# Values past stationary probabilities: the attention products of a hybrid decoder trunk with a query per output row

## The chip, the cores and the metric

The kernel runs on one core of a Trainium2 chip. The metric is device time in microseconds (us) of one execution. The engines are TensorE (PE; its weight loads are listed apart as PEld), VectorE (DVE), ScalarE (ACT), GpSimd (POOL) and SyncE (SP), which issues most transfers.

## What is computed

Two layers are run over 512 rows of width 1024, in float32. Each layer has three groups of attention heads: A (sliding window of 128, 8 heads with a sink), B (4 heads that see the 128 keys an indexer chose) and C (4 heads, latent attention). All have values of width 64. Their outputs are concatenated and go through one output projection; then come a layer norm and a mixture of 16 experts of which each row uses two. What the change touches is the end of each softmax; from the reference, for group C:

```python
s = jnp.where(causal[None, None], s, -jnp.inf)
p = jax.nn.softmax(s, axis=-1)
return jnp.einsum('bhts,bshd->bthd', p.astype(v.dtype), v)
```

## The kernel before

**Order of the work.** Nothing is scheduled by the hardware or a compiler. Every piece of work is a Python generator that yields steps: an engine (or two to choose from), a guessed cost and a function that issues the instructions. A planner (`Flow.run`, L144) picks at each turn the step that can start first by its guesses, with a small weight on a priority (`PRIO`, L84), and issues it. Each engine then runs its instructions strictly in that order, and the waits between the engines follow from the data. A wrong guess does not change the order; it only makes an engine wait, or arrive late, at run time.

**Stages of a layer.** The input projection (`s_project`, L538) runs in five column chunks; each product is made of three float32r products (`mm3`, L284 to 287). Rotary embedding and transposes (`turn`, L433, whose transposes are on L440) bring queries and keys into shape. An indexer scores keys for group B (`s_index`, L705) and 16 rounds of MAX8 and MATCH_REPLACE8 on DVE (L745, L746) choose 128 of them. Sixteen quads of heads (`s_quad`, L753) do the attention: a quad is four heads for one block of 128 queries. A has eight quads, B and C four each. Then come the output projection (`s_wout`, L916, again L285 to 287), the norm and the router (`s_router`, L1021, whose small products are on L1034), the table of rows (L1133 is filler work that PE does while it waits there) and twelve passes over the experts (L1619 and L1648), whose weights stream in from memory.

**One quad before.** The number of keys nk is 128 or 256 in group A, and 128, 256, 384 and 512 in B and C for the four blocks; nj is nk/128. The scores are products on PE (L786). DVE adds the mask and takes the minimum (L772), ACT takes the exponential and the row sums (L799), DVE the reciprocal of the sums (L804). Then each of the four heads' probabilities is multiplied by the reciprocal of its row's sum, on DVE (L808) or on ACT (L809), whichever the planner expects to end first. Blocks of 128 by 128 probabilities are transposed on PE (L440), up to four into one bank, and copied out (`evac`, ACT on L281 or DVE on L282). The products with the values follow (L834). There the values, 128 keys by 64, are the stationary operand, and the transposed probabilities, 128 keys by 128 queries, move past them:

```python
b = (hh % 2) * 64
T.matmul(po[b:b + 64, (hh // 2) * P:(hh // 2 + 1) * P], vs[hh][j], q[:, j], start=j == 0, stop=j == nj - 1)
```

An output has its 64 columns of values as rows; two heads of a pair write the lower and the upper 64 rows, so each product uses half of the columns of PE's array. The products of a quad are issued in one step of four heads where nk is at most 256 (`per` is 2, so a transposing step takes two heads), and in two steps of two heads otherwise. The result already stands as the output projection wants it, with features on the rows, and is copied into `mix` (quads of A) or split into its two float32r parts (B and C, L850 on ACT and L851 on DVE).

In the trace a float32 product is two matmul records, each with a weight load of its own; a transpose and a float32r product are one record each.

Of the kernel before, what the change touches and what calls it, by code (L numbers as in the profile page):

```python
# [10 lines left out]
AF = mybir.ActivationFunctionType  # L11
OP = mybir.AluOpType
# [4 lines left out]
P = 128  # L17
# [180 lines left out]
def body(tc, sb, pp, dr, x, w_in, attn_sinks, c_q_norm_g, c_kv_norm_g, w_uq, w_ukv, w_out, ln1_g, ln1_b,  # L198
         w_router, router_bias, w_gate, w_up, w_down, ln2_g, ln2_b, rope, out):
    nc = tc.nc  # L200
    V, A, G, T, SY = nc.vector, nc.scalar, nc.gpsimd, nc.tensor, nc.sync
# [25 lines left out]
    def fixed(*shape):  # L227
        n = 1
        for d in shape:
            n *= d  # L230
        return view(take_f(n), *shape)
# [14 lines left out]
    def sel(i):  # L246
        o = ((i + 1) * i // 2 - 1) * P
        return aux.of(F32)[:, o:o + (i + 1) * P]
# [12 lines left out]
    def st(eng, cost, fn, after=None):  # L261
        return Step([(eng, cost, fn)], after)

    def pe(cost, fn, after=None):
        return st("T", cost, fn, after)

    def ve(n, fn, after=None, fast=False):
        return st("V", 0.07 + n / (1920 if fast else 960), fn, after)

    def ac(n, fn, after=None, extra=0):  # L270
        return st("A", 0.07 + n / 1200 + 0.093 * extra, fn, after)
# [22 lines left out]
    ident = fixed(P)  # L294
# [103 lines left out]
    WT = Slots([fixed(512) for _ in range((NF - used[0]) // 512)])  # L398
# [8 lines left out]
    def rshape(w, *shape):  # L407
        n = 1
        for d in shape:
            n *= d  # L410
        v = w[:, :n]
        if len(shape) == 2:
            v = v.rearrange("p (a b) -> p a b", b=shape[1])
        if len(shape) == 3:
            v = v.rearrange("p (a b c) -> p a b c", b=shape[1], c=shape[2])
        return v
# [16 lines left out]
    def turn(src, n, after=None):  # L433

        got = yield Take(PS)
        ps = got[1].rearrange("p (a b) -> p a b", b=P)

        def tr():
            for j, s in enumerate(src):
                T.transpose(ps[:n, j, :], s, ident)  # L440
        t = yield pe(0.107 * len(src), tr, after)
        return got, ps[:n, :len(src), :], t

    def turned(got, q, te, dst, dst_lo=None):

        n = q.shape[1] * P
        if dst_lo is None:
            t = yield evac(n, dst, q, [te])
        else:
            t = yield ac(n, lambda: A.activation(dst, q, AF.Copy), [te])  # L450
            t = yield ve(n, lambda: V.tensor_tensor(dst_lo, q, dst.bitcast(F32), op=OP.subtract), [t])  # L451
        PS.put(got, t)
        return t
# [24 lines left out]
    def layer(l, xready, prev_free):  # L478
# [274 lines left out]
        def s_quad(q, i, need, qs, ks, vs, mask, nk, scale, c0, sink=None):  # L753

            for e in need:
                yield e
            if mask is None:
                mask = sel(i)
            nj = nk // P
            per = 2 if nk <= 256 else 1  # L760
            nm, sm, es = smalls["nm", q], smalls["sm", q], smalls.get(("es", q))
            s = [None] * 4
            gots = yield Take(WS, 4 // per)
            groups = [(0, 2), (1, 3)] if per == 2 else [(h,) for h in range(4)]
            ahead = []

            def scores():
                g_, got, tq = ahead.pop(0)
                v, ps = rshape(gots[g_][1], per, nk), got[1]
                for a, h in enumerate(groups[g_]):  # L770
                    s[h] = v[:, a]
                    t = yield ve(nk + 60, lambda: V.tensor_tensor_reduce(  # L772
                        out=v[:, a], in0=ps[:, a * nk:(a + 1) * nk], in1=mask, op0=OP.add, op1=OP.min, scale=-scale,
                        scalar=3e38 if sink is None else sink[:, h:h + 1], accum_out=nm[:, h:h + 1]), [tq])
                PS.put(got, t)
                return t

            both = qs[0].shape[0] == 64
            for g0 in range(0, len(groups), 2 if both else 1):
                banks_ = yield Take(PS, 2 if both else 1)  # L780

                def qk():
                    for a in range(per):
                        for j, got in enumerate(banks_):
                            h = groups[g0 + j][a]
                            T.matmul(got[1][:, a * nk:(a + 1) * nk], qs[h], ks[h], start=True, stop=True)  # L786
                tq = yield pe(per * 4 * nk / 2400 + 0.2 * both, qk, [])
                for j, got in enumerate(banks_):
                    ahead.append((g0 + j, got, tq))
                while len(ahead) > (0 if both else 1):  # L790
                    t = yield from scores()
            while ahead:
                t = yield from scores()
            if sink is not None:
                t0 = yield ve(4, lambda: V.tensor_tensor(es, nm, sink, op=OP.subtract), [t])
                t0 = yield ac(4, lambda: A.activation(es, es, AF.Exp), [t0])
            ts_ = []
            for h in range(4):
                ts_.append((yield ac(nk, lambda: A.activation(s[h], s[h], AF.Exp, bias=nm[:, h:h + 1], scale=-1.0,  # L799
                                                              accum_out=sm[:, h:h + 1]), [t], 3)))  # L800
            t = ts_[-1]
            if sink is not None:
                t = yield ve(4, lambda: V.tensor_tensor(sm, sm, es, op=OP.add), [t])
            t = yield ve(4, lambda: V.reciprocal(sm, sm), [t])  # L804
            tn = []
            for h in range(4):
                tn.append((yield Step([
                    ("V", 0.12 + nk / 1920, lambda: V.tensor_scalar(s[h], s[h], sm[:, h:h + 1], None, op0=OP.mult)),  # L808
                    ("A", 0.19 + nk / 1200, lambda: A.activation(s[h], s[h], AF.Copy, scale=sm[:, h:h + 1]))], [t])))  # L809
            gpo, po = None, None  # L810
            ahead = []
            for h in range(0, 4, per):
                src = [s[h + a][:, j * P:(j + 1) * P] for a in range(per) for j in range(nj)]
                b_ = yield from turn(src, P, [tn[h + per - 1]])
                gp = yield Take(WT)
                pT = rshape(gp[1], 4, P)[:, :len(src)]
                te = yield from turned(*b_, pT)
                if per == 1:
                    WS.put(gots[h], te)
                for a in range(per):  # L820
                    ahead.append((h + a, gp if a == per - 1 else None, pT[:, a * nj:(a + 1) * nj], te))
                if len(ahead) < (4 if per == 2 else 2):
                    continue

                if po is None:
                    gpo = yield Take(PS)
                    po = gpo[1]

                def pv():
                    for x in range(0, len(ahead), 2):  # L830
                        for j in range(nj):
                            for hh, _, q, _ in ahead[x:x + 2]:
                                b = (hh % 2) * 64
                                T.matmul(po[b:b + 64, (hh // 2) * P:(hh // 2 + 1) * P], vs[hh][j], q[:, j], start=j == 0, stop=j == nj - 1)  # L834
                tp = yield pe(len(ahead) / 2 * nj * 0.22 + 0.2, pv, [v[3] for v in ahead])
                for _, g_, _, _ in ahead:
                    if g_ is not None:
                        WT.put(g_, tp)
                ahead.clear()
            if per == 2:  # L840
                for g_ in gots:
                    WS.put(g_, te)
            qsl = slice(i * P, (i + 1) * P)
            qq = po[:, :2 * P].rearrange("p (a b) -> p a b", a=2)
            if q < 8:
                yield E("idx")
                t = yield evac(2 * P, mix[:, c0:c0 + 2, qsl], qq, [tp])
            else:
                yield E("mm", len(chunks) - 1)
                yield ac(2 * P, lambda: A.activation(xh()[:, c0:c0 + 2, qsl], qq, AF.Copy), [tp])  # L850
                t = yield ve(2 * P, lambda: V.tensor_tensor(xl(c0, c0 + 2, qsl), qq, xh()[:, c0:c0 + 2, qsl].bitcast(F32),  # L851
                                                            op=OP.subtract))
                flow.set(E("mix", c0 // 2, i), t)
            PS.put(gpo, t)
            flow.set(E("quad", q), t)

        for i in range(NT):
            qi = slice(i * P, (i + 1) * P)
            k0 = max(0, i - 1) * P
            nk = (i + 1) * P - k0  # L860
# [8 lines left out]
            nk = (i + 1) * P  # L869
# [955 lines left out]
```

## Time and profile before

| | |
|---|---|
| median of 3 runs | 833.25 us (833.22 to 834.62) |
| the profiled execution: its time | 835.47 us |
| its span, first to last instruction | 833.7 us |
| mean granted clock of TensorE in it | 0.995 |
| busy over the span: PE / DVE / ACT | 97% / 64% / 41% |

The span is what all rows of the trace add up to; the profiled execution's own time has 1.8 us around it. Busy time of an engine is the union of its instructions. Matmuls overlap each other: one of them is listed with some 0.27 us although the next may start 0.1 us later, so the price of a matmul in a stream is read from the starts, not from the durations. A time such as "idle before" is that of the engine which waited, with the instruction that released it.

### The profile page before, as it was taken

The numbers are of one execution on the slowest core, as the hardware profiler recorded it, in microseconds if no ns is written. First come the engines' busy times: TensorE is split into PE (matmuls) and PEld (weight loads), VectorE is DVE, ScalarE is ACT, GpSimd is POOL, SyncE is SP. The second block draws the span as 40 slices with busy tenths as digits, with TensorE's granted clock in tenths as the row PEclk, the third lists the DMA queues.
The fourth block names the chain that finished last, engine by engine and source line by source line (L and its number), as shares of the span: only waits on it lengthen the run. The fifth ranks groups of instructions, "written<-read, shape, count | busy, mean of one in ns | idle before, by whom it ended". The sixth has DMA issues, their size and how long they took to land. (4 is left out here: it accounts for less than half of the span.)

```text
span 833.7 us, 15557 instructions
## 1 busy us (share of the span) xinstructions
PE 806.0 (97%) x5960; PEld 521.7 (63%) x5960; DVE 537.5 (64%) x1588; ACT 338.2 (41%) x852; POOL 103.2 (12%) x133
## 2 busy tenths in 40 slices
PE   7999999999999999999999999999999999999995
PEld 7878896667885333333597889776688743333332
DVE  5799999974477341123998999989644854211257
ACT  4433656974232222223155265577632232222211
POOL 1010102000003111100211001110000121111004
PEclk9999999999999999999999999999999999999998
DMA  8421350064575999997434217111762699999762
GB/s 267 151 84 49 112 207 27 26 207 172 177 262 196 353 373 377 370 366 276 176 88 164 77 51 242 37 52 27 273 232 101 213 333 366 367 375 370 278 274 101
DMA packets 118848, 171.91 MB, mean 206 GB/s; under 512 B 12005, under 2 KB 95461, under 8 KB 118768
## 3 DMA queue, kind: packets, MB, share of 16 engines
q1 hardware_dynamic: 112720, 156.12, 54.6%
q0 software_dynamic: 6048, 14.73, 4.9%
q8 instruction: 48, 0.79, 0.4%
q14 instruction: 32, 0.26, 0.1%
HBM read 152.96 MB, written 25.17 MB: 214 GB/s over the span
## 5 line engine op out<-in xcount | busy, mean ns | idle before, releaser
L285 PE MATMUL bank<-ring,ra 128*128 128x512 f32 (+4 forms) x448 | 167.0, 373 | 0.5 <-ACT fa L604 0.5
L1648 PE MATMUL bank<-fa,ra 128*32 128x512 f32 x1080 | 160.0, 592 | 0.2
L286 PE MATMUL bank<-ring,xl 128*128 128x512 f32 (+4 forms) x448 | 157.6, 352 | 0.9 <-DVE xl L451 0.9
L287 PE MATMUL bank<-ring,ra 128*128 128x512 f32 (+4 forms) x448 | 158.0, 353 | 0.0
L281 ACT ACTIVATE fa<-bank 128x256 f32<-128x256 f32 (+3 forms) x172 | 86.1, 514 | 108.2 <-PE bank L440 80.2
L1524 DVE TENSOR_TENSOR fa<-fa,bank 128x256 f32<-128x256 f32 x24 | 10.1, 421 | 160.3 <-ACT fa L1523 160.3
L1648 PEld LDWEIGHTS bank<-fa,ra 128*32 128x32 f32 x1080 | 47.6, 109 | 76.6 <-issue 65.6
L285 PEld LDWEIGHTS bank<-ring,ra 128*128 128x128 f32 x448 | 85.0, 190 | 14.9 <-issue 7.1
L287 PEld LDWEIGHTS bank<-ring,ra 128*128 128x128 f32 x448 | 84.8, 189 | 8.2
L286 PEld LDWEIGHTS bank<-ring,xl 128*128 128x128 f32 x448 | 85.2, 190 | 7.4 <-DVE xl L451 1.3
L1619 PE MATMUL bank<-fa 128*32 128x512 f32 x504 | 80.0, 595 | 1.4 <-DVE fa L282 0.6
L440 PE MATMUL bank<-fa 128*128 128x128 f32 (+1 forms) x456 | 71.9, 282 | 7.4 <-DMA fa<-in_x_dram 5.7
L473 ACT ACTIVATE ring<-fa 128x1024 fp32r<-128x1024 f32 (+4 forms) x56 | 49.5, 898 | 55.4 <-PE bank L286 49.8
L440 PEld LDWEIGHTS bank<-fa 128*128 128x128 f32 (+1 forms) x456 | 55.4, 144 | 24.4 <-issue 10.5
L1523 ACT ACTIVATE fa<-bank 128x256 f32<-128x256 f32 x24 | 9.2, 385 | 151.1 <-PE bank L1648 144.5
L1648 PE MATMUL bank<-ring,ra 128*32 128x512 f32 x360 | 67.1, 592 | 0.0
L474 DVE TENSOR_TENSOR ring<-fa,ring 128x1024 fp32r<-128x1024 f32 (+4 forms) x56 | 58.0, 1043 | 7.4 <-ACT ring L473 7.3
L1514 DVE TENSOR_SCALAR ra<-bank,fa 128x128 f32<-128x128 f32 x110 | 41.8, 408 | 27.9 <-ACT ra L1513 24.5
L746 DVE MATCH_REPLACE8 aux<-fa,aux 128x256 f32<-128x256 f32 (+2 forms) x96 | 51.9, 545 | 0.0
L745 DVE MAX8 fa<-aux 128x8 f32<-128x256 f32 (+2 forms) x96 | 50.6, 551 | 0.1
L1513 ACT ACTIVATE ra<-bank,fa 128x128 f32<-128x128 f32 x82 | 33.7, 458 | 41.1 <-DVE ra L1514 36.6
L786 PE MATMUL bank<-fa 64*128 64x256 f32 (+7 forms) x256 | 47.4, 413 | 0.0
(218 smaller groups left out, 1235.5 us busy)
## 6 DMA issues: line engine op xcount, KB each, us to landing
fa<-in_w_gate_dram SPq DMA_DIRECT2D x45, 512.0 KB, 9.8
fa<-in_w_up_dram SPq DMA_DIRECT2D x45, 512.0 KB, 9.8
fa<-in_w_down_dram SPq DMA_DIRECT2D x21, 1024.0 KB, 10.5
xl<-in_w_down_dram SPq DMA_DIRECT2D x9, 1024.0 KB, 10.5
fa<-in_w_out_dram SPq DMA_DIRECT2D x8, 1024.0 KB, 5.7
yd<-fa SPq DMA_DIRECT2D x16, 512.0 KB, 8.7
ring<-in_w_gate_dram SPq DMA_DIRECT2D x15, 512.0 KB, 6.8
ring<-in_w_up_dram SPq DMA_DIRECT2D x15, 512.0 KB, 11.9
```

What stands on the lines that cost most here:

```text
L281: return Step([("A", 0.05 + n / 1200, lambda: A.activation(dst, src, AF.Copy)), ("V", 0.12 + n / 960, lambda: V.tensor_copy(dst, src))], a ...
L285: T.matmul(ps, xh, wh, start=start, stop=False)
L286: T.matmul(ps, xl, wh, start=False, stop=False)
L287: T.matmul(ps, xh, wl, start=False, stop=stop)
L440: T.transpose(ps[:n, j, :], s, ident)
L473: yield Step([("A", 0.09 + n / 1200, lambda: A.activation(hv, raw, AF.Copy))], None)
L474: t = yield ve(n, lambda: V.tensor_tensor(lv, raw, hv.bitcast(F32), op=OP.subtract))
L745: yield ve(nk, lambda: V.max(m8, sc))
L746: yield ve(nk, lambda: V.match_replace(sc, m8, sc, MARK))
L786: T.matmul(got[1][:, a * nk:(a + 1) * nk], qs[h], ks[h], start=True, stop=True)
L1619: T.matmul(a[1][cs], ht[:, j, cs], E("raw", e, 2).got[1][:, j, n * 512:(n + 1) * 512], start=j == 0, stop=j == 1)
L1648: T.matmul(acc[1][cs], gh[:, 4 * u + j, cs], E("raw", e, u).got[1][:, j], start=u + j == 0, stop=u + j == 4)
```

## The change

The quad's end is turned around. The exponentials are transposed as they are, without the division. In the products the transposed exponentials (128 keys by 128 queries) are the stationary operand and the values (128 keys by 64) move; an output has a query per row and, for four heads, 256 columns. These rows are multiplied by the reciprocals in one DVE instruction per quad, which writes them over the last buffer of transposed exponentials; two transposes on PE turn them into the other half of the same bank, and from there the result is copied as before. The steps of the products now come once per transposing step.

```diff
--- before.py
+++ after.py
@@ -802,46 +802,43 @@
             if sink is not None:
                 t = yield ve(4, lambda: V.tensor_tensor(sm, sm, es, op=OP.add), [t])
             t = yield ve(4, lambda: V.reciprocal(sm, sm), [t])
-            tn = []
-            for h in range(4):
-                tn.append((yield Step([
-                    ("V", 0.12 + nk / 1920, lambda: V.tensor_scalar(s[h], s[h], sm[:, h:h + 1], None, op0=OP.mult)),
-                    ("A", 0.19 + nk / 1200, lambda: A.activation(s[h], s[h], AF.Copy, scale=sm[:, h:h + 1]))], [t])))
-            gpo, po = None, None
-            ahead = []
+
+            td = t
+            gpo, po, spare = None, None, None
             for h in range(0, 4, per):
                 src = [s[h + a][:, j * P:(j + 1) * P] for a in range(per) for j in range(nj)]
-                b_ = yield from turn(src, P, [tn[h + per - 1]])
+                b_ = yield from turn(src, P, [ts_[h + per - 1]])
                 gp = yield Take(WT)
                 pT = rshape(gp[1], 4, P)[:, :len(src)]
                 te = yield from turned(*b_, pT)
                 if per == 1:
                     WS.put(gots[h], te)
-                for a in range(per):
-                    ahead.append((h + a, gp if a == per - 1 else None, pT[:, a * nj:(a + 1) * nj], te))
-                if len(ahead) < (4 if per == 2 else 2):
-                    continue
-
                 if po is None:
                     gpo = yield Take(PS)
                     po = gpo[1]
 
                 def pv():
-                    for x in range(0, len(ahead), 2):
+                    for a in range(per):
                         for j in range(nj):
-                            for hh, _, q, _ in ahead[x:x + 2]:
-                                b = (hh % 2) * 64
-                                T.matmul(po[b:b + 64, (hh // 2) * P:(hh // 2 + 1) * P], vs[hh][j], q[:, j], start=j == 0, stop=j == nj - 1)
-                tp = yield pe(len(ahead) / 2 * nj * 0.22 + 0.2, pv, [v[3] for v in ahead])
-                for _, g_, _, _ in ahead:
-                    if g_ is not None:
-                        WT.put(g_, tp)
-                ahead.clear()
+                            T.matmul(po[:, (h + a) * 64:(h + a + 1) * 64], pT[:, a * nj + j], vs[h + a][j], start=j == 0, stop=j == nj - 1)
+                tp = yield pe(per * nj * 0.115, pv, [te])
+                if h + per < 4:
+                    WT.put(gp, tp)
             if per == 2:
                 for g_ in gots:
                     WS.put(g_, te)
+
+            rows = rshape(gp[1], 4, 64)
+            t = yield ve(2 * P, lambda: V.tensor_tensor(rows, po[:, :2 * P].rearrange("p (a b) -> p a b", b=64), sm[:, :, None].to_broadcast([P, 4, 64]),
+                                                        op=OP.mult), [tp, td])
+
+            def tr():
+                for j in range(2):
+                    T.transpose(po[:, (2 + j) * P:(3 + j) * P], gp[1][:, j * P:(j + 1) * P], ident)
+            tp = yield pe(0.214, tr, [t])
+            WT.put(gp, tp)
             qsl = slice(i * P, (i + 1) * P)
-            qq = po[:, :2 * P].rearrange("p (a b) -> p a b", a=2)
+            qq = po[:, 2 * P:].rearrange("p (a b) -> p a b", a=2)
             if q < 8:
                 yield E("idx")
                 t = yield evac(2 * P, mix[:, c0:c0 + 2, qsl], qq, [tp])
```

## Rows read from the trace of the kernel before

**Rows 1.** The page, busy time over the whole span: share, number of instructions

```profile
PE 806.0 (97%) x5960; PEld 521.7 (63%) x5960; DVE 537.5 (64%) x1588; ACT 338.2 (41%) x852; POOL 103.2 (12%) x133
```

**Rows 2.** Windows: both attention stretches and the output projection behind the first, all engines

```profile
core 0: us, PE busy (x) PEld busy (x) DVE busy (x) ACT busy (x) POOL busy (x), PEclk, DMA share, GB/s
70.00:200.00 130.00, 127.47 (x887) 99.21 (x886) 112.20 (x386) 85.30 (x258) 13.32 (x21) 1.00 0.35 117
200.00:245.00 45.00, 44.79 (x287) 38.40 (x284) 24.67 (x72) 14.17 (x23) 2.32 (x4) 1.00 0.53 182
...
478.00:612.00 134.00, 131.49 (x908) 102.25 (x907) 117.08 (x397) 87.29 (x256) 13.85 (x23) 1.00 0.35 120
```

**Rows 3.** The longest wait of PE, first attention stretch: total us, times, longest

```profile
PE bank L834 <- DVE ring L282: 1.0, 2, 0.7
```

**Rows 4.** Windows of L834 alone, then its groups with the idle time before them

```profile
70.00:200.00 130.00, 20.72 (x272) 15.12 (x272) 1.00 0.35 117
478.00:612.00 134.00, 19.97 (x272) 14.90 (x272) 1.00 0.35 120
...
L834 PE MATMUL bank<-fa 128*64 128x128 f32 x290 | 26.7, 279 | 0.7 <-DVE fa L282 0.4 <-ACT fa L281 0.3
...
L834 PE MATMUL bank<-ring,fa 128*64 128x128 f32 x254 | 24.3, 281 | 2.3 <-DVE ring L282 1.8 <-ACT ring L281 0.5
```

**Rows 5.** Timeline of PE: one step of L834 between projections (start, duration)

```profile
93.49 1.10 PE L834 MATMUL bank<-fa 128*64 128x128 f32 x16
94.52 0.46 PE L285 MATMUL bank<-ring,ra 128*128 128x416 f32 x1
```

**Rows 6.** Timeline of PE: the router's products, 128x128 stationary, 16 columns moving

```profile
230.42 0.39 PE L287 MATMUL bank<-ring,ra 128*128 128x512 f32 x1
230.65 0.96 PE L1034 MATMUL bank<-fa 128*128 128x16 f32 x8
231.46 0.49 PE L285 MATMUL bank<-ring,ra 128*128 128x512 f32 x1
231.78 0.40 PE L286 MATMUL bank<-ring,xl 128*128 128x512 f32 x1
```

**Rows 7.** Timeline of PE: products with 128x128 stationary, 128 columns moving

```profile
657.28 3.84 PE L1247 MATMUL bank<-fa 128*128 128x128 f32 x32
660.95 0.55 PE L1262 MATMUL bank<-rv,sl 128*128 128x24 bf16 x16
```

**Rows 8.** Timeline of PE: four transposes between projections

```profile
91.63 0.36 PE L287 MATMUL bank<-ring,ra 128*128 128x416 f32 x1
91.82 0.60 PE L440 MATMUL bank<-fa 128*128 128x128 f32 x4
92.18 0.43 PE L285 MATMUL bank<-ring,ra 128*128 128x416 f32 x1
92.45 0.35 PE L286 MATMUL bank<-ring,xl 128*128 128x416 f32 x1
```

**Rows 9.** Windows of L808, then of L809, in the two attention stretches

```profile
sum 264.00, DVE 26.95; mean DVE 13.47
...
sum 264.00, ACT 18.45; mean ACT 9.22
```

**Rows 10.** Who waited longest for L808, and then for L809: total us, times

```profile
  PEld bank L440: 1.5, 4
...
  PEld bank L440: 1.0, 2
  PEld bank L834: 0.7, 3
```

**Rows 11.** Timeline of DVE: a subtraction that reads 256 columns of a bank, a MAX8

```profile
164.37 0.42 DVE L851 TENSOR_TENSOR xl<-bank,ra 128x256 fp32r<-128x256 f32 x1
164.71 0.69 DVE L745 MAX8 fa<-aux 128x8 f32<-128x512 f32 x1
```

**Rows 12.** The chain that ended last: the price of float32 products of 512 columns

```profile
807.54 1.72 PE bank L1724 x4
```

## The prediction, made before the change was run

> **What bounds the kernel now.** The page comes first: PE is busy in 97% of the span, DVE in 64%, ACT in 41% [rows 1]. Busy does not yet mean that PE is the limit, since a listed matmul overlaps its neighbours; so the next view is the windows by stage. In the two attention stretches, 70 to 200 and 478 to 612 us, PE is busy 127.5 of 130 and 131.5 of 134 us; DVE is close behind with 112.2 and 117.1 us, ACT is not [rows 2]. What PE waits for there is small: its longest entry is 1.0 us in all [rows 3], and the whole idle time of both stretches is 2.5 + 2.5 = 5.0 us [rows 2]. The output projection behind it leaves PE idle for 0.2 of 45 us [rows 2], so it has nothing in which a late start could be caught up. TensorE's granted clock is 1.00 in these stretches, the upper of its two levels (2.4 GHz), and this change gives no reason for it to fall. So the change has to be priced in PE time first, and DVE and ACT time count only where PE is found waiting for them.
>
> **What leaves PE.** A layer has 136 products of probabilities with values: 8 for the two quads of A with one key block, 48 for its six with two, 40 each for B and C (4 heads times 1, 2, 3 and 4 blocks). Two layers and two records each make 544 records, which is what the windows of L834 count (272 and 272). They keep PE busy for 20.72 + 19.97 = 40.7 us, and PE stood idle for 0.7 + 2.3 = 3.0 us just before some of them: 43.7 us in all, 80 ns for a record [rows 4]. A step of 16 records takes 1.03 us until the next instruction starts, 64 ns each [rows 5]; the rest of the 80 is the short steps and the waits. It is below what 128 moving columns cost alone, since the two heads of a pair run in two halves of the array at once.
>
> **What comes to PE: the products.** There are 544 records again, now with a full 128 by 128 stationary operand and 64 moving columns. The trace has no such form, but it has both neighbours. With 16 moving columns, the router's eight records take 0.81 us until the next starts, and that one takes 0.32 us to its successor where the one ahead took 0.23: 0.90 us, 112 ns each [rows 6]. With 128 moving columns, 32 records take 3.67 us, 115 ns each [rows 7]. A form that costs the same with 16 and with 128 moving columns is not priced by its moving columns; what the two share is the stationary operand. For 64 columns I take 112 ns: 544 x 0.112 = 60.9 us. The bounds are 0.101 (0.81/8) and 0.115: 54.9 and 62.6 us.
>
> The Trainium skill, page "TensorE: Matmul & The Clock Gate", section "Back-to-back issue gap", gives the gap of warm matmuls as N/2.4 + 2.5 ns, so 64 columns would cost about half of what 128 do; by it the 60.9 us would be some 31 us, an estimate from that page and rows 7. The two neighbours above speak against using it here.
>
> **What comes to PE: the transposes.** Two for each of 32 quads, 64 in all. Four transposes take 0.36 us until the next instruction, which is itself 0.08 us late (0.27 us to its successor against 0.19 for the one ahead), 0.11 each [rows 8]: 7.0 us.
>
> The net of PE's own work is 60.9 + 7.0 - 43.7 = **+24.2 us**.
>
> **What leaves and comes to DVE and ACT.** The 128 divisions go: 27.0 us of DVE and 18.5 us of ACT [rows 9]. One multiplication per quad comes to DVE: 256 columns read from a bank with a second operand, for which the subtraction of that shape, 0.42 us [rows 11], stands: 32 x 0.42 = 13.4 us. DVE is relieved by 13.6 us, ACT by 18.5. What hides this work today is PE; were PE not the limit, it would be worth up to the 13.6 us. On PE's path only what it waited for these divisions counts: 1.5 us behind L808 and 1.0 + 0.7 behind L809 [rows 10], 3.2 us of weight-load waits, part of which lay beside running matmuls. I take 2 (bounds 0 and 3.2).
>
> **Waits.** The transposing of a quad can start a reciprocal and a division earlier, and with PE later against the other engines, data will stand ready more often: of the 5.0 us of idle time I take 3 as filled (bounds 0 and 5.0 less the 2 above). New handoffs are made: per quad the multiplication waits for the last product and the transposes wait for the multiplication, 32 of them, and the steps of products go from 40 to 80 (12 quads of a layer from one to two, 4 from two to four). The nearest row for a handoff is the idle time before L834, 3.0 us for 40 steps, 0.075 us each [rows 4]; 72 new ones would be 5.4 us. The planner puts other work between, and it guesses 0.115 us for a product against two records of 0.112 measured above, so PE will run behind its plan and find its data; I take 1.4 (bounds 0 and 5.4). What queues behind the multiplication on DVE is mainly the rounds of MAX8 and MATCH_REPLACE8, and DVE has been given 13.6 us for that. The bank of outputs is held longer, from the first product to the copy; the planner sees this and I cost it at nothing as long as it finds other work for PE, which it does in nearly all of the stretch [rows 2].
>
> **Sum.** +24.2 - 2 - 3 + 1.4 = +20.6 us, half in each layer. Against the profiled execution (835.47 us, 833.7 of them span) that is 856.1; it stood 2.2 us above the median of 833.25, so I forecast 833.25 + 20.6 = 853.9, **854 us**. By its bounds the sum runs from 54.9 + 7.0 - 43.7 - 5.0 = +13.2 to 62.6 + 7.0 - 43.7 + 5.4 = +31.3.
>
> **Rivals.**
> *A. The moving columns set the price, and the kernel gets faster.* The place is the products' stream in the two attention stretches. Float32 products of 512 columns cost 1.72/4 = 0.43 us a record [rows 12], in proportion 54 ns for 64 columns. The sum is then 544 x 0.054 + 7.0 - 43.7 = -7.3 us, with nothing from the waits: 826 us. It decides below (43.7 - 7.0)/544 = 67 ns a record. The equal prices at 16 and 128 columns [rows 6, 7] speak against it. This is the outcome of the rule cited above, and it has a chance of 0.06.
>
> *B. DVE is the hidden limit, and its relief pays half.* DVE is busy in 86 to 87% of the attention stretches [rows 2], so some of what looks like PE work may be PE spread out to DVE's pace. Then the 13.6 us come back: 24.2 - 13.6 = +10.6, 844 us. Against it: PE's waits name DVE for only a few tenths at a time [rows 3]. 0.10.
>
> *C. The new wait stands bare.* The two transposes stand at the head of PE's queue while the multiplication waits behind a MAX8 (0.69 us) and then takes 0.42 us [rows 11]. With half a MAX8 ahead on average it is 0.77 us a quad; bare in half of the 32 quads it is 12 us more: 866 us. It speaks for this that DVE works on the choosing of keys while the quads run; against it, that planned work stands between. 0.10.
>
> *D. The price doubles.* If a product with all columns of the array to itself costs twice what it costs today, it is 43.7 more instead of 17.2: 854 + 26 = 880 us. The Trainium skill, page "TensorEngine Tiling (Array Packing)", section "Theoretical Speedup", gives up to 2x for the packing that is undone here, the rule that speaks most against the change. The two neighbours put the ratio at 60.9/43.7 = 1.4 instead [rows 4, 6, 7]. 0.02.
>
> **How the numbers follow.** The forecast has 0.72, A 0.06, B 0.10, C 0.10, D 0.02. The range from 843 to 866 us holds B's 844, the forecast between most of its bounds (+13.2 is 846, +31.3 is 865) and the lower half of C. About 0.2% is what a measurement of this kernel can tell from no change. A gives faster, and a tail of the forecast's case in which the new order of the work happens to be good adds 0.01: 0.07. The same gets 0.02, from B with more relief than reckoned; slower has the rest, 0.91.
>
> **What would show it.** In the changed kernel's profile: records of the products with 128 by 128 stationary and 64 moving columns at starts 112 ns apart, and no half-array form left; two transposes per quad behind one DVE multiplication of about 0.42 us; no DVE or ACT instruction of a division; DVE's busy total down by some 14 us and ACT's by some 18; both attention stretches longer by 8 to 13 us each with PE still without gaps, and all later stages as long as before. The prediction is wrong if the products stand closer than 67 ns, if the output projections begin no later than before, or if PE shows idle times of half a microsecond and more before the new transposes.

## The result, and the profile after

The changed kernel takes **863.74 us** (median of 4 runs, 861.13 to 865.72) against 833.24 (4 runs): 30.5 us more, a ratio of 1.0359 with a 95% interval of 1.0341 to 1.0378. The forecast was 854 us with a range of 843 to 866. The direction and the range held; the loss is half as large again as the 20.6 us forecast.

The page's busy times after, to be set against [rows 1]:

```profile
PE 833.8 (97%) x6024; PEld 562.2 (65%) x6024; DVE 526.4 (61%) x1520; ACT 327.6 (38%) x821; POOL 98.4 (11%) x136
```

PE has 64 records more (the new transposes) and 27.8 us more busy time; DVE has lost 11.1 us and ACT 10.6. Both are less than the 14 and 18 forecast; for ACT one reason is that the planner now gives it 211 copies out of banks instead of 203 (L281). Busy time tells little of why, so next the windows by stage, to be set against [rows 2]. The edges are moved to where the stages now lie: attention and output projection of layer 0, then of layer 1.

```profile
70.00:207.00 137.00, 135.62 (x904) 115.11 (x902) 106.02 (x354) 76.36 (x237) 13.14 (x24) 1.00 0.30 101
207.00:251.00 44.00, 42.71 (x234) 36.09 (x233) 21.73 (x56) 13.36 (x21) 1.67 (x3) 1.00 0.49 171
488.00:637.00 149.00, 146.11 (x947) 123.68 (x946) 109.70 (x360) 81.39 (x242) 11.69 (x23) 0.99 0.32 109
637.00:677.00 40.00, 37.18 (x198) 31.14 (x195) 18.47 (x52) 11.82 (x19) 1.67 (x3) 0.91 0.40 137
```

Two things are new. In the output projections PE is now idle for 1.3 of 44 and 2.8 of 40 us, where it was idle for 0.2 of 45 [rows 2] and, in layer 1, for 0.2 of 40 (the row below). And in layer 1 the granted clock is below full, 0.99 and 0.91.

```profile
612.00:652.00 40.00, 39.79 (x264) 34.35 (x263) 21.43 (x69) 9.92 (x18) 2.32 (x4) 1.00 0.54 180
```

The starts in the trace say where the 30.2 us by which the span grew arise. The last product of an output projection starts at 251.0 instead of 239.7 us in layer 0; from the first product of layer 1 to its last output projection are 248.1 us instead of 228.6; everything else, the expert passes above all, is as long as before to within 0.6 us. So layer 0 lost 11.3 us, close to the 10.3 forecast for a layer, and **layer 1 lost 19.5**. In this execution, what was missed is in layer 1. Summed over both layers from each record's start to the next instruction's, the products with the values have grown by 18.6 us and the new transposes are 7.7; the projections (L285 to 287) have grown by 6.3 us and the router's products, with the wait behind them, by 2.3.

The price of the products is read from PE's timeline, one step of four products (eight records) behind two of the new transposes and one between other work:

```profile
96.28 0.35 PE L287 MATMUL bank<-ring,ra 128*128 128x416 f32 x1
96.47 1.07 PE L823 MATMUL bank<-fa 128*128 128x64 f32 x8
97.38 0.61 PE L440 MATMUL bank<-fa 128*128 128x128 f32 x4
...
98.97 0.38 PE L837 MATMUL bank<-fa 128*128 128x128 f32 x2
99.18 1.00 PE L823 MATMUL bank<-fa 128*128 128x64 f32 x8
100.00 0.43 PE L285 MATMUL bank<-ring,ra 128*128 128x416 f32 x1
```

Eight records take 0.91 us until the transposes start: 114 ns each. Over the whole trace the median from one such record to the next is 112 ns, the price taken from the router's products [rows 6].

The transposes and the multiplication of the rows, as groups of their line (idle time last) and in windows (the L832 sum is the 32 multiplications on DVE):

```profile
L837 PE MATMUL bank<-fa 128*128 128x128 f32 x44 | 8.7, 278 | 0.0
L837 PE MATMUL bank<-fa,ring 128*128 128x128 f32 x20 | 3.8, 281 | 0.0
...
sum 290.00, DVE 13.59; mean DVE 6.80
```

PE was never listed as idle before the new transposes; the planner did put other work between. The multiplication costs 13.59/32 = 0.42 us, as forecast.

In layer 1's output projection the timeline of PE shows this:

```profile
646.44 0.39 PE L287 MATMUL bank<-ring,ra 128*128 128x512 f32 x1
646.67 0.96 PE L1031 MATMUL bank<-fa,ring 128*128 128x16 f32 x8
649.84 0.50 PE L285 MATMUL bank<-ring,ra 128*128 128x512 f32 x1 [2.21 <-ACT ring L473]
650.18 0.43 PE L286 MATMUL bank<-ring,xl 128*128 128x512 f32 x1
651.22 0.80 PE L287 MATMUL bank<-ring,ra 128*128 128x512 f32 x1 [0.61 <-DVE ring L474]
651.81 0.63 PE L285 MATMUL bank<-ring,ra 128*128 128x512 f32 x1
```

The projection waits for the split of its second half of weights (L473 and L474, which write ring cells). Just before, the router's products (L1031) read "fa,ring": the router's turned rows stand in a buffer that was lent out of that ring. Before the change that line read "fa" alone [rows 6], in both layers. In layer 0 the same two splits end the 1.3 us of idle time (0.8 and 0.5), although the router's rows stand in no lent buffer there; that wait was not followed up.

### The profile page after: what moved, and what is told of

Read it like the earlier page. It is cut to its first block, busy times and chain, and to the rows that moved or that the text cites. A ratio compares the mean times of both kernels' runs of the same rounds, so it can differ in the third digit from the quotient of the medians.

```text
span 863.9 us, 15694 instructions
## 1 busy us (share of the span) xinstructions
PE 833.8 (97%) x6024; PEld 562.2 (65%) x6024; DVE 526.4 (61%) x1520; ACT 327.6 (38%) x821; POOL 98.4 (11%) x136
## 5 line engine op out<-in xcount | busy, mean ns | idle before, releaser
L285 PE MATMUL bank<-ring,ra 128*128 128x512 f32 (+4 forms) x448 | 170.4, 380 | 3.5 <-ACT ring L473 3.0
L287 PE MATMUL bank<-ring,ra 128*128 128x512 f32 (+4 forms) x448 | 159.7, 357 | 1.1 <-DVE ring L474 1.1
L281 ACT ACTIVATE fa<-bank 128x512 f32<-128x512 f32 (+3 forms) x187 | 93.1, 515 | 147.2 <-PE bank L440 105.1
L285 PEld LDWEIGHTS bank<-ring,ra 128*128 128x128 f32 x448 | 86.0, 192 | 18.5 <-issue 6.8
L287 PEld LDWEIGHTS bank<-ring,ra 128*128 128x128 f32 x448 | 85.7, 191 | 10.5 <-DVE ring L474 2.0
L440 PE MATMUL bank<-fa 128*128 128x128 f32 (+1 forms) x520 | 78.5, 279 | 6.3 <-DMA fa<-in_x_dram 5.6
L440 PEld LDWEIGHTS bank<-fa 128*128 128x128 f32 (+1 forms) x520 | 62.3, 145 | 18.6 <-issue 7.5
L473 ACT ACTIVATE ring<-fa 128x1024 fp32r<-128x1024 f32 (+4 forms) x56 | 49.9, 898 | 59.5 <-PE bank L286 46.9
L474 DVE TENSOR_TENSOR ring<-fa,ring 128x1024 fp32r<-128x1024 f32 (+4 forms) x56 | 58.0, 1042 | 21.3 <-ACT ring L473 21.2
L799 ACT ACTIVATE fa<-fa 128x256 f32<-128x256 f32 (+3 forms) x100 | 49.3, 497 | 0.0
L823 PEld LDWEIGHTS bank<-fa 128*128 128x128 f32 x358 | 45.2, 193 | 6.2 <-ACT fa L281 1.5
```

Source lines behind the costliest of these rows:

```text
L281: return Step([("A", 0.05 + n / 1200, lambda: A.activation(dst, src, AF.Copy)), ("V", 0.12 + n / 960, lambda: V.tensor_copy(dst, src))], a ...
L285: T.matmul(ps, xh, wh, start=start, stop=False)
L287: T.matmul(ps, xh, wl, start=False, stop=stop)
L473: yield Step([("A", 0.09 + n / 1200, lambda: A.activation(hv, raw, AF.Copy))], None)
L474: t = yield ve(n, lambda: V.tensor_tensor(lv, raw, hv.bitcast(F32), op=OP.subtract))
```

## The experiments

**The stationary load or the moving columns?** Each product is split in two of 32 columns.

```diff
-    for j in range(nj):
-        T.matmul(po[:, (h + a) * 64:(h + a + 1) * 64], pT[:, a * nj + j], vs[h + a][j], ...)
+    for c, j in [(c, j) for c in (0, 32) for j in range(nj)]:
+        o = (h + a) * 64 + c
+        T.matmul(po[:, o:o + 32], pT[:, a * nj + j], vs[h + a][j][:, c:c + 32], ...)
```

> The changed kernel with each product of 64 moving columns split into two of 32: the same columns, twice the stationary loads. Theory (the price of a record is its 128 by 128 stationary operand, 112 ns whatever moves): 544 more records at 112 ns, 61 us more, 918 to 928 us. Rival (the moving columns set the price): 864 to 869 us.

Measured: 966.06 us, 102.3 more than the changed kernel. The moving columns do not set the price: the rival's 864 to 869 us is far off. The time is also above the theory's 918 to 928 us; the excess over 61 us is clock, as the mean clock has it. Windows of this kernel, with the granted clock as the third figure from the end:

```profile
170.00:200.00 30.00, 28.91 (x149) 25.25 (x150) 12.34 (x43) 8.91 (x31) 0.00 (x0) 0.66 0.05 18
200.00:220.00 20.00, 20.00 (x143) 17.78 (x141) 6.91 (x20) 5.65 (x16) 0.00 (x0) 0.83 0.39 132
220.00:240.00 20.00, 19.72 (x103) 14.64 (x101) 6.46 (x16) 8.11 (x21) 0.54 (x1) 0.75 0.30 106
640.00:680.00 40.00, 38.97 (x204) 34.00 (x204) 14.76 (x56) 15.32 (x54) 0.00 (x0) 0.66 0.08 27
```

The mean clock over its 962.2 us is 0.951, which is 2 x 0.049 x 962 = 94 us at the lower level (1.2 GHz); some 8 of them lie after the last product, as in the kernel before (0.995). The other 86 us at half the rate lose 43, an estimate from these figures: 61 + 43 = 104, next to the measured 102. Where the clock is full a record still stands 112 ns from the next, where it is halved 213, with 32 columns as with 64. The step ahead of a fall is seen in PE's timeline, a short wait and then a stream of such records:

```profile
172.57 1.97 PE L824 MATMUL bank<-fa,ring 128*128 128x32 f32 x16 [0.78 <-DVE ring L282]
...
181.34 3.46 PE L824 MATMUL bank<-fa 128*128 128x32 f32 x16
```

16 records take 1.81 us (to the next start at 174.38) in the first row and 3.27 us in the second (to 184.61).

**The transposes, doubled.**

```diff
-    for j in range(2):
+    for j in (0, 1, 0, 1):
         T.transpose(po[:, (2 + j) * P:(3 + j) * P], gp[1][:, j * P:(j + 1) * P], ident)
```

> The changed kernel with the two transposes of the rows issued twice, one pair behind the other: 64 more transposes and no new wait. Theory (PE has no slack there): 64 x 0.11 = 7 us more, 868 to 873 us. Rival (PE's added work lies partly in time in which it waits anyway): under 3 us more.

Measured: 869.76 us, 6.0 more (by the scatter of four runs each, some 3 to 9), 94 ns a transpose. From start to start the row transposes take 14.4 us instead of 7.7. PE's added work shows almost in full, so at this place PE has no slack in the changed kernel.

**The ring cell.** The router's rows take only buffers that are not lent.

```diff
-    gw = yield Take(WT)
+    gw = yield Take(WT, None, 0, 99)
     xq = rshape(gw[1], 4, P)
```

> The changed kernel; the router's turned rows take no buffer that was lent by the ring of split weights. Theory 1 (in the second layer the split of the output weights waits for a ring cell in which the router's rows stand, PE is idle for 2.8 us there and its clock falls): the idle time goes, 3 us less, and up to 8 less with the clock, 856 to 861 us. Theory 2 (the ring cell is not what the split waited for): 863 to 866 us.

Measured: 858.40 us (856.26 to 861.75), 5.3 less, of which the scatter of four runs each leaves some 1 to 9. The same 20 us in layer 1, first of the changed kernel, then of this one:

```profile
640.00:660.00 20.00, 17.18 (x81) 14.11 (x81) 7.48 (x13) 5.48 (x10) 0.56 (x1) 0.83 0.38 126
```

```profile
640.00:660.00 20.00, 20.00 (x112) 17.02 (x111) 7.39 (x19) 6.03 (x10) 1.12 (x2) 1.00 0.52 184
```

The 2.8 us of idle time are gone, and so is the fall of the clock, 0.83 to 1.00. An earlier fall of the changed kernel, ahead of this wait at 620 us, is absent here as well; why is not shown. The cause of the wait itself is settled: a lent buffer that the planner gave to the router. That it did so because the quads now end later is argued, not shown. The wait in layer 0 (0.8 and 0.5 us) is still there in this kernel.

**The guess for a product, raised, and then both mends at once.**

```diff
-    tp = yield pe(per * nj * 0.115, pv, [te])
+    tp = yield pe(per * nj * 0.225, pv, [te])
```

> The changed kernel with the planner's guess for a product raised from 0.115 to 0.225 us, twice the 0.112 of a record; nothing but the order of the work changes. Theory 1 (the loss over the forecast comes from a plan that takes PE to be earlier than it is, so that the second layer's output projection waits for its weights): 5 to 9 us less, 855 to 859 us. Theory 2 (only the price of PE's own work counts): within 2 us of 863.7.

Measured: 860.25 us (858.51 to 861.52), 3.5 less, between the two theories. It is another order of the work, in which the waits of both output projections are gone; the window of layer 1:

```profile
637.00:677.00 40.00, 39.79 (x262) 34.38 (x261) 23.37 (x71) 11.86 (x21) 2.32 (x4) 1.00 0.52 178
```

> The changed kernel with both mends, the guess of 0.225 us and the router's rows out of the lent ring. If they mend the same wait in the second layer: 856 to 860 us, no better than the better of the two alone. If they mend two things: 852 to 856 us. In neither case near 833, since PE's own work, 60 us of products and 7 us of transposes, is unchanged.

Measured: 861.27 us (861.03 to 863.37), above both forecasts. The two do not add up. In this kernel's profile PE is idle for 0.1 us in the output projections of both layers, so the wait is mended here too; the 3.5 us by which the experts' products (L1648 of the kernel before) take longer from start to start than in the ring cell's kernel, 172.2 against 168.7, undo the gain. Why they differ is open, but for a fall of the clock near 275 us (0.91 in the mean of the 20 us from 260). Between the medians of the three mended kernels lie 1 to 3 us, about what their runs scatter.

**What the division is worth, alone.** The kernel before without it; the outputs are scaled by 1/8 in the copies.

```diff
-    tn.append((yield Step([
-        ("V", ..., lambda: V.tensor_scalar(s[h], s[h], sm[:, h:h + 1], None, op0=OP.mult)),
-        ("A", ..., lambda: A.activation(s[h], s[h], AF.Copy, scale=sm[:, h:h + 1]))], [t])))
...
-    b_ = yield from turn(src, P, [tn[h + per - 1]])
+    b_ = yield from turn(src, P, [ts_[h + per - 1]])
```

> The kernel before without the division (left out; the attention outputs are scaled by 1/8 in the copies instead): what the 27 us of DVE and 18 us of ACT are worth by themselves. Theory (PE is the limit): 1 to 4 us less, 829 to 832 us. Rival (DVE is the hidden limit): 10 to 14 us less, 819 to 823 us.

Measured: 823.80 us, 10.2 less (ratio 0.9875, 0.9859 to 0.9892). This is beyond the theory's 1 to 4 us. The windows of both attention stretches, and then the groups of the products with their idle time, to be set against [rows 2, 4]:

```profile
70.00:190.00 120.00, 119.91 (x867) 95.07 (x866) 100.90 (x338) 77.67 (x239) 12.99 (x24) 1.00 0.36 120
470.00:600.00 130.00, 129.97 (x906) 101.68 (x905) 105.11 (x350) 79.09 (x238) 13.18 (x24) 1.00 0.37 127
...
L829 PE MATMUL bank<-fa 128*64 128x128 f32 x372 | 30.8, 278 | 0.0
L829 PE MATMUL bank<-ring,fa 128*64 128x128 f32 x172 | 16.9, 281 | 0.0
```

PE is idle for 0.1 us in both stretches together, where it was 5.0. But 10.2 us were gained (9.0 to 11.8 by the interval). Summed over the trace from each record's start to the next instruction's, the products take 35.9 us here (66 ns a record) and 40.8 in the kernel before, and the transposes of L440 68.5 and 72.0. So more time went than the views list as idle. One reason can be read off: a record is listed with 0.27 us while in a stream the next starts after 0.06 to 0.11, so a wait of up to 0.2 us is covered by the tail of the record ahead, and a longer one is listed too short by about as much. The order of the work has changed little at this place: the products stand in 36 separate streams instead of 38. How much of the rest is such covered waits was not taken apart.

The 66 ns are not the price inside a stream. The two heads of a pair, one in each half of the array, are seen here in one of the longest streams of this kernel (start, duration):

```profile
160.35 0.27 PE L829 MATMUL bank<-ring,fa 128*64 128x128 f32 x1
160.36 0.27 PE L829 MATMUL bank<-fa 128*64 128x128 f32 x1
160.46 0.27 PE L829 MATMUL bank<-ring,fa 128*64 128x128 f32 x1
160.47 0.27 PE L829 MATMUL bank<-fa 128*64 128x128 f32 x1
```

Two records take 0.11 us, 55 ns each; the median over the trace is 55 too, here and in the kernel before. The rest is paid at the ends of a stream. From its last record to the next instruction are 0.20 us, and from a transpose ahead to its first record as well, where one transpose follows another after 0.11 us; that makes some 0.1 us more on entering and 0.1 on leaving.

**Its load or its place?** The 128 divisions are issued behind the transposes, where nobody waits for them; the outputs are scaled by 1/8 as above.

> As the kernel before without its division (outputs scaled by 1/8 in the copies), but the 128 divisions are issued all the same, behind the transposes that read the exponentials, where nobody waits for their results: the load on DVE and ACT without its place in a quad's chain. Theory 1 (the 10 us that fell with the division are load, which delays what stands behind it on DVE and ACT): 831 to 835 us. Theory 2 (they are the division's latency between reciprocal and transposes): 823 to 826 us.

Measured: 828.29 us (827.66 to 829.84). Between the two: of the 10.2 us about 4.5 are the load on DVE and ACT, and 5.7 its place between the reciprocal and the transposes, each to within 1 to 2 us. From start to start the products take 35.6 us, as without the division, and the transposes of L440 72.8, as with it.

**The swap without the late division.** The changed kernel with the division back in its old place; DVE only copies the rows.

> The changed kernel with the division of the probabilities put back (128 instructions on DVE or ACT, as before) and the rows only copied by DVE, not multiplied: the swap of the operands alone. Theory (PE is the limit, so the work taken from DVE and ACT is worth next to nothing): 863 to 868 us. Rival (DVE is the hidden limit and its relief held the loss down): the 27 us of DVE and 18 us of ACT come back and cost 10 us or more, 874 us or above.

Measured: 879.97 us (874.83 to 883.50), 16 more. Taken alone this looks like the rival, DVE as the hidden limit. The windows show something else:

```profile
150.00:162.00 12.00, 9.85 (x73) 7.52 (x71) 9.88 (x47) 9.44 (x25) 0.62 (x2) 1.00 0.00 1
162.00:190.00 28.00, 26.87 (x107) 21.38 (x106) 14.32 (x48) 12.91 (x45) 0.00 (x0) 0.51 0.21 76
590.00:610.00 20.00, 17.45 (x90) 13.70 (x88) 14.30 (x59) 13.41 (x43) 0.76 (x2) 0.74 0.08 27
```

PE waits (2.2 of 12 us, the longest 1.4 us for a division, the row below), and then the clock is at half for 27 us:

```profile
PE bank L440 <- DVE fa L809: 1.4, 1, 1.4
```

The last two stretches are 28 us at a mean clock of 0.51 and 20 us at 0.74, so 27 + 10 us at the lower level; at half the rate that loses some 19 us. Without them this execution, 882.47 us, would stand at 863 or 864; the other three, reckoned by their mean clocks less 8 us at the lower level behind the last product, at about 867. These estimates lie where the theory had it (863 to 868), some 2 to 6 us above the changed kernel's own runs at a mean clock of 0.995 (861.1 and 861.9). So this run does not measure DVE's relief: most of its loss is clock, in stretches that follow such waits. That the waits are what made it fall was not tried apart.

**Three attempts to beat the kernel before.** The divisions may also go to POOL:

> The kernel before; the planner may also give a head's division to POOL, which is idle for most of the span, at a guess of 0.2 us and 3.2 ns a column. Correct in full. If the load on DVE and ACT is what the division costs, the part that POOL takes comes back: 825 to 831 us. If its latency is what costs, POOL's longer instruction gains nothing: 832 to 840 us.

Measured: 834.63 us, ratio 1.0003 (0.9994 to 1.0013): nothing. POOL took only 22 of the 128 (0.40 to 0.83 us each); of the 4.5 us that the load is worth, 22/128 are 0.8 us, and the interval reaches almost as far. So this run does not decide between load and latency.

The planner's guesses for a division raised to the measured durations:

> The kernel before with the planner's guesses for a division raised to what the trace shows (0.35 us on DVE, 0.50 us on ACT for 256 columns, where it guessed 0.25 and 0.40). If part of the 10 us that the division costs is a plan that starts transposes before their operands are there: 829 to 832 us. If the work itself has to be done somewhere in the chain whatever the plan says: within 2 us of 833.3.

Measured: 833.66 us, ratio 0.9999 (0.9990 to 1.0008): no difference.

The late division with the half-array products kept, the reciprocals transposed by PE instead of the rows:

```diff
+    yield po_(0.9, lambda: G.tensor_copy(..., sm[:, :, None].to_broadcast([P, 4, 64])), [t_rec, te])
+    flow.set(fac, (yield from transposed([v[:, c * P:(c + 1) * P] for c in range(2)], P, ...)))
...
-    t = yield evac(2 * P, mix[:, c0:c0 + 2, qsl], qq, [tp])
+    t = yield ve(2 * P, lambda: V.tensor_tensor(mix[:, c0:c0 + 2, qsl], qq, ff, op=OP.mult), [tp, tf])
```

> The late division without the swap, correct in full: the kernel before with its half-array products, the exponentials undivided, and the reciprocals spread by POOL, transposed by PE (two transposes a quad, 7 us in all) and multiplied in as the outputs are copied. If the 10 us that the division's place cost come back against 7 us of transposes: 829 to 833 us, below both kernels. Rival (the chain behind the last product, POOL's spreading and the transposes, makes a new wait at the end of each quad): 836 to 845 us.

Measured: 838.99 us, 5.7 more, as the rival had it. From start to start the products take 37.3 us instead of 40.8, so part of the division's price came back; the transposes of L440, the 64 new ones among them, take 82.6 instead of 72.0, 10.6 more where 7 were reckoned. PE's longest new wait is for the copies behind transposes:

```profile
PE bank L440 <- ACT fa L281: 2.2, 2, 1.1
```

Which part of the loss this is was not separated.

Two heads past one stationary block, half the records and the same columns:

> The kernel before, whose quads of groups A and B with at most 256 keys move two heads past one stationary value block, 256 columns instead of twice 128, in each half of the array: the same columns with half the records and loads. If records and loads cost something even in paired form (66 ns a record in a stream, where its columns alone are 54): 829 to 832 us. If only the columns count there: within 1 us of 833.3.

Measured: 833.47 us, ratio 0.9998 (0.9988 to 1.0008). Of 544 records 136 fewer gain nothing that can be measured. That fits the 55 ns inside a paired stream: the 66 ns of the expectation hold the ends of the steps, and above the 54 of the columns a record in the stream has nothing left to give. No version that computes everything was found to beat the kernel before.

## Why the prediction was right, and where not

**What bounds the kernel: right.** Doubling 64 transposes cost 6.0 of the 7 us reckoned; PE's work adds to the time. But DVE and ACT counted for more than the waits that were found listed: in the kernel before, the division cost 10.2 us.

**The price of the products: right.** 112 ns a record was forecast from neighbours with 16 and with 128 moving columns, and 112 was found with 64 and with 32. Rival A is refuted by the split into halves: halving the moving columns left the price of a record as it was. The Trainium skill ("TensorE: Matmul & The Clock Gate", "Back-to-back issue gap") gives N/2.4 + 2.5 ns as the gap of an isolated matmul and says itself that at small N this counts too little in a stream of weight loads and matmuls, which the prediction left out. The runs agree with that warning: 112 ns at 64 and at 32 columns, where the formula would give 29 and 16. Summed from start to start the products take 59.4 us against 60.9 forecast, the row transposes 7.7 against 7.0.

**What leaves PE: mis-sized, hidden by an opposite error.** I took 43.7 us for the old products, waits included, and 2 us of relief from the division. Without the division these products take 35.9 us, and the division's going is worth 10.2 instead of the "I take 2 (bounds 0 and 3.2)" and the 3 us of filled idle time. Put right, the sum is 59.4 + 7.7 - 35.9 - 10.2 = +21.0 us, by chance next to the +20.6 forecast: the old products carried part of the wait that I then credited too little for. That the two errors cancel is luck. The error was to take the listed idle time as all that the division costs.

**The waits: the step that failed.** "I take 1.4 (bounds 0 and 5.4)" for new waits, looked for before the new transposes, where there are none. I had costed buffers held longer at nothing, with only the bank of outputs in mind. Of the 9.5 us between +21.0 and +30.5, 5.3 (some 1 to 9 by the scatter) go with the wait in layer 1's output projection and the clock around it, as the ring experiment shows: the planner lends the router a cell that the weights need. Between the profiled executions of the two kernels, the slowest of the one and the fastest of the other, layer 1 is shorter by 7.5 us, and 8.0 us are gone from the projections' and the router's products; the span of the latter is 20.8 us above that before, next to the forecast. So between these two the excess lies in the projections, in waits and clock, and not in the quads. The 4 us between the medians that the ring does not explain were not taken apart.

**The clock.** "This change gives no reason for it to fall" was wrong: the changed kernel's own profile has it at a mean of 0.83 for 20 us of layer 1.

**The other rivals.** B (844 us) did not come about, though its price was not far off: the division is worth 10.2 us by its absence, half of it for its place in the chain and not for DVE's load. C did not occur where it was placed; a bare wait came elsewhere. D's 880 us did not come; the ratio of new to old products is 59.4/35.9 = 1.65, between the 2x named there and the 1.4 that I had set against it from figures with waits in them. Inside a stream the price did double, from 55 to 112 ns a record. The kernel loses less because its paired streams were short and each paid some 0.2 us at its ends, which the full-array products do not: from one of them to a transpose, or from a transpose to one of them, are 0.11 us.

## What to carry to other kernels

The price of a small float32 product behind a full 128 by 128 stationary operand is set by that operand: from 16 to 128 moving columns it was the same 112 to 115 ns a record, at 512 it was 430. So take it from a product in the trace with the same stationary shape and no more than 128 columns. Idle time listed before matmuls is a lower bound of the waiting, since each record's tail covers a short wait; the price in a stream and the price of getting in and out of it are two figures, to be read from the starts; to size what a removed instruction is worth, run the kernel once without it. Another order of the work can hand a stage different buffers, so look at which stage takes what another one needs.

## What was not expected of the hardware

TensorE's granted clock went to its lower level in stretches where the engine was listed as fully busy: 20.00 of 20 us at a mean clock of 0.83 in the kernel with halved products. What it did before the falls shown here was a stream of float32 products with few moving columns behind full stationary loads, with single waits of 0.3 to 2.2 us between. Which of these makes the clock fall was not tried apart. In the kernel before no fall was seen until after the last products. The changed kernel is thus liable to a loss that its count of instructions does not show: two of its four runs, with mean clocks of 0.991 and 0.990, took 865.7 and 865.6 us, the two at 0.995 took 861.1 and 861.9.
